# Fewer raw weight slots, a prepared bias table, and products on TensorE that nothing reads, in a streaming encoder layer

## The chip, the cores and the metric

The kernel runs on one core of a Trainium2 chip. A core has five engines that run their own instruction streams: TensorE (PE, with its weight loads listed as PEld), VectorE (DVE), ScalarE (ACT), GpSimd (POOL) and SyncE (SP), which here issues nearly all DMA transfers. The metric is the device time of one execution in microseconds. The kernel before took 1180.17 us, the median of three runs (1178.12 to 1184.04).

## The reference

One layer of an encoder: three groups of attention heads read the same normalised input through one input projection and are merged by one output projection. The call handles a prompt of 2048 rows and a sample batch of 8 x 16 = 128 rows, which have cached keys and values. The core of it:

```python
qa, ka, va, ga, qb, kb, vb, gb, qm, gm = _project(yp, g_pre[l], w_in[l])   # RMSNorm, then one matmul
oa = _band_attention(..., 8 chunks to the left, _relpos_bias(rel_bias_a[l], d), None)   # A: 6 heads x 64
ob = _band_attention(..., 2 chunks to the left, ALiBi, sink_b[l])                       # B: 6 q, 2 kv heads
om = _attn_core(qm, mk, mv, None, None, None)                                           # M: 4 heads, 256 tokens
yp = x + _rmsnorm(concat(oa*silu(ga), ob*silu(gb), om*silu(gm)) @ w_out[l], g_post[l])
```

In branch A a row of chunk c sees the keys of chunks c - 8 to c, 576 keys, and to each score a learned bias is added that depends on the head and on the distance, clipped at 128. The sample rows run through the same projections and attend to 512 cached keys and their own 16 (A), to 128 and 16 (B) and to 256 memory tokens (M). All is float32, D_MODEL is 1024.

## The kernel before, in words

**Precision and weights.** Each float32 product is done as three products of split numbers: a value is split in a high part and the low rest, and high x high, low x high and high x low are summed (`PASSES`). So each weight tile of 128x1024 is prepared by `load_w` (L145): SP starts a DMA into a raw tile (`wraw`, pool `wrawp`), ACT makes the high half (L153), and DVE and POOL in turn make the low half (L154) in a tile `whl`, of which there are three. The pool `wrawp` has three slots, and not for weights alone: the cached keys of the sample rows (`kta` L736, `ktb` L824) and two residual rows at the very end use the same ring. The slots are given out in the order in which the program asks for them, and a request waits until the last reader of the slot's former tile is done.

**Groups and order.** The prompt is worked on in 4 groups of 512 rows; group 0 carries the 128 sample rows too. In each group one lane of dense steps (projections to queries, keys and gates as `psT`, L213; to values, the memory's among them, and outputs as `psN`, L226) and one lane of attention steps are woven together: `DENSE` and `ATTENTION` list the steps, `AFTER` what must precede them, and `PACE` sets how much dense work is recorded per unit of attention. In group 0 the dense lane is V0 Pa0 Pa1 V1 Pb0 K0 and so on, the attention lane M0 M1 Sa0 Aa0 Sa1 Aa1 Sb0 Ab0: V are value weights, Pa and Pb the projections of a head pair, K0 the keys of branch B, Sa and Sb the sample rows' attention, Aa and Ab the prompt's. A scheduler then sets the order on each engine from costs that it assumes; each engine runs its own list in that order.

**The head.** `first_rows` (L477) loads the first 640 rows in eight blocks of 128 input features, scales each (`xn`, high part by ACT, L489, low by DVE, L490) and asks for the first two weights. `biases` (L349) loads the sinks and builds a row of 767 biases by distance for each head, which goes to DRAM (`e_d`). `bands` (L369) copies each head's row 128 times to DRAM (`skew_d`), so that a read with a row step of 767 instead of 768 gives a bias that depends on row minus column (`toeplitz`).

**Where the bias is read.** For the sample rows `sample_a` (L719) puts the bias of a head pair together from 17 small transfers (`nbs`). For the prompt `weigh` in `attn_a` loads a 128x640 tile for each head (`nbA`, L757); POOL then writes 1e30 into the two corners of 64x64 that a chunk may not see (L758, L759). DVE subtracts this bias from the scores. PSUM tiles of the tag `pt` (pool `p_t`) serve transposes and, in the head, some projections.

## Time and profile before

| What | Value |
|---|---|
| median of the runs | 1180.17 us (1178.12 to 1184.04) |
| the profiled execution | 1177.05 us, span 1175.3 us |
| mean granted TensorE clock | 0.987 |
| busy: PE, PEld | 1126.3 us (96%), 1019.6 us (87%) |
| busy: DVE, ACT, POOL | 810.9 us (69%), 729.4 us (62%), 301.1 us (26%) |
| instructions of POOL | 243, of them 48 memsets on `nbA` |
| PE products `psT` (L213) | 2400, 522.1 us busy |
| weight transfers `wraw` | 128 of 512 KB, median 3.6 us from issue to landing |

A timeline row gives the start, the length, the engine, the line with its operation, output and inputs with their shapes, how many instructions are taken together, and in brackets the idle time of the engine just before and what ended it. A stage window gives the busy time of each engine within a stretch of the span and the TensorE clock that was granted in it.

### The profile page before, as it was taken

To read this page: it belongs to the slowest core of one execution; us is meant where nothing else is said; L and a number is where in the kernel's file an instruction comes from. 1 tells how busy PE (TensorE), PEld (TensorE's weight loads), DVE (VectorE), ACT (ScalarE), POOL (GpSimd) and SP (SyncE) were. 2 spreads that over 40 slices of the span, in tenths; PEclk is the share of its full clock that TensorE was granted. 3 is DMA by queue.
4 is the path that set the end of the run, shared out by engine and by line. 5 is a ranking of instruction groups with operands and counts; after the bars stand their busy time and mean duration, and the time that the engine had idled before them with its cause. 6 is when DMAs were issued, how large, how long until landed. Compare 5 with 4: busy or idle time off the path is not lost.

```text
span 1175.3 us, 20987 instructions
## 1 busy us (share of the span) xinstructions
PE 1126.3 (96%) x7794; PEld 1019.6 (87%) x7794; DVE 810.9 (69%) x1875; ACT 729.4 (62%) x1688; POOL 301.1 (26%) x243
## 2 busy tenths in 40 slices
PE   7899999899899999999999999999999999999997
PEld 6889899799589988998789988988889988898797
DVE  7738766677775347677988337678987337678865
ACT  7646555666575566566886455567876456567762
POOL 4210210120321461221411451221411541212211
PEclk9999999899899999999999999999999999999899
DMA  7663445324721494233330394333321483232222
GB/s 274 221 226 136 155 158 206 113 83 132 266 95 43 159 332 167 92 108 116 116 95 24 108 368 164 93 124 104 113 94 37 125 297 97 77 115 84 76 68 100
DMA packets 62237, 163.42 MB, mean 139 GB/s; under 512 B 8108, under 2 KB 19378, under 8 KB 62136
## 3 DMA queue, kind: packets, MB, share of 16 engines
q1 hardware_dynamic: 58392, 152.66, 38.5%
q0 software_dynamic: 3744, 9.44, 2.7%
q8 instruction: 61, 1.00, 0.3%
q14 instruction: 40, 0.33, 0.1%
HBM read 140.95 MB, written 23.48 MB: 140 GB/s over the span
## 4 chain that ended last, share of the span: by engine, by line
PE 69%; DVE 10%; issue 8%; ACT 8%; DMA 3%; POOL 2%; SPq 1%; DVEq 0%; POOLq 0%; ACTq 0%
PE psT L213 31%; PE psN L226 20%; PE pt L273 4%; PE oa L286 4%; PE sa L267 4%; DVE sh L235 2%; ACT whl L153 1%; POOL whl L154 1%; PE ob L286 1%; DMA xt<-in_x_p 1%; DVE whl L154 1%; PE ss L384 1%; PE om L286 1%; DVE sbm L689 1%; PE so L420 1%
## 5 line engine op out<-in xcount | busy, mean ns | idle before, releaser
L213 PE MATMUL psT<-xn,whl 128*128 128x512 f32 (+2 forms) x2400 | 522.1, 367 | 13.7 <-ACT whl L153 5.7
L213 PEld LDWEIGHTS psT<-xn,whl 128*128 128x128 f32 x2400 | 408.3, 190 | 75.5 <-ACT whl L153 5.7
L154 POOL TENSOR_TENSOR whl<-wraw,whl 128x1024 fp32r<-128x1024 f32 x63 | 154.1, 2446 | 350.5 <-ACT whl L153 301.4
L226 PE MATMUL psN<-whl,sh 128*128 128x256 f32 x1296 | 164.0, 284 | 7.3 <-POOL whl L154 5.3
L226 PEld LDWEIGHTS psN<-whl,sh 128*128 128x128 f32 x1296 | 157.3, 190 | 10.0 <-POOL whl L154 5.7
L153 ACT ACTIVATE whl<-wraw 128x1024 fp32r<-128x1024 f32 (+1 forms) x132 | 138.3, 1047 | 26.1 <-PE psN L226 16.4
L226 PE MATMUL psN<-whl,xn 128*128 128x256 f32 x1080 | 145.1, 284 | 2.9 <-ACT stgN L652 1.1
L226 PEld LDWEIGHTS psN<-whl,xn 128*128 128x128 f32 x1080 | 134.4, 189 | 6.3 <-issue 1.6
L235 DVE TENSOR_TENSOR sh<-pt,sh 128x512 fp32r<-128x512 f32 (+2 forms) x206 | 122.2, 625 | 13.0 <-ACT sh L234 12.0
L234 ACT ACTIVATE sh<-pt 128x512 fp32r<-128x512 f32 (+2 forms) x206 | 103.6, 547 | 34.8 <-PE pt L273 26.4
L775 ACT ACTIVATE sba<-sba,sta 128x640 f32<-128x640 f32 (+2 forms) x96 | 73.1, 762 | 57.8 <-DVE sta L773 57.3
L154 DVE TENSOR_TENSOR whl<-wraw,whl 128x1024 fp32r<-128x1024 f32 (+1 forms) x69 | 94.9, 1375 | 19.4 <-ACT whl L153 18.7
L665 POOL TENSOR_TENSOR mo<-sums,gr 128x256 f32<-128x256 f32 (+1 forms) x38 | 37.6, 989 | 234.7 <-DVE sums L294 208.8
L773 DVE CUSTOM_DVE_ANT_0 sba<-sa,nbA 128x640 f32<-128x640 f32 (+2 forms) x96 | 70.7, 737 | 28.8 <-PE sa L267 27.8
L286 PE MATMUL oa<-sh 128*128 128x256 f32 (+1 forms) x504 | 75.1, 281 | 1.8 <-DVE sh L235 0.9
L286 PEld LDWEIGHTS oa<-sh 128*128 128x128 f32 x504 | 68.4, 192 | 5.0 <-DVE sh L235 1.9
L273 PE MATMUL pt<-ident,sba 128*128 128x128 f32 x420 | 64.6, 276 | 3.4 <-DVE sh L235 2.6
L526 DVE TENSOR_TENSOR mo<-psN,gpost 128x256 f32<-128x256 f32 x52 | 21.9, 422 | 61.6 <-ACT junk L525 61.4
L778 DVE TENSOR_SCALAR sba<-sba,sta 128x640 f32<-128x640 f32 (+2 forms) x96 | 59.4, 619 | 2.7
L267 PE MATMUL sa<-sh,qr 128*128 128x320 f32 (+2 forms) x240 | 52.0, 327 | 4.4 <-DVE sta L773 2.3
L273 PEld LDWEIGHTS pt<-ident,sba 128*128 128x128 f32 x420 | 48.7, 141 | 7.2 <-DVE sh L235 3.4
L858 ACT ACTIVATE sbb<-sbb,stb 128x256 f32<-128x256 f32 (+1 forms) x96 | 47.3, 494 | 11.4 <-DVE stb L856 11.2
(285 smaller groups left out, 1572.8 us busy)
## 6 DMA issues: line engine op xcount, KB each, us to landing
wraw<-in_wt SPq DMA_DIRECT2D x128, 512.0 KB, 3.6
xr<-in_x_p SPq DMA_DIRECT2D x16, 512.0 KB, 5.3
nbA<-skew_d SPq DMA_DIRECT2D x24, 320.0 KB, 2.9
vta<-in_cva SPq DMA_DIRECT2D x12, 512.0 KB, 5.0
xt<-in_x_p SPq DMA_DIRECT2D x12, 512.0 KB, 4.9
out_y_p<-mo SPq DMA_DIRECT2D x12, 512.0 KB, 4.0
vctx<-sh SPq DMA_DIRECT2D x9, 512.0 KB, 5.0
kctx<-sh SPq DMA_DIRECT2D x9, 512.0 KB, 4.1
```

The source lines that it names most:

```text
L153: act.activation(hl[:, 0, m], raw[:, m], AF.Copy)
L154: eng.tensor_tensor(hl[:, 1, m], raw[:, m], hl[:, 0, m].bitcast(F32), ALU.subtract)
L213: pe.matmul(ps[:, :n], w[:, a, k * 128:(k + 1) * 128], src[:, b, k, c0:c0 + n], start=(i == 0), stop=(i == 23))
L226: pe.matmul(ps[:, :256], stat(a, k), w[:, b, (k % 4) * 256:(k % 4 + 1) * 256], start=(k == ks[0] and i == 0), stop=(k == ks[-1] and i == 2))
L234: act.activation(hi, src, AF.Copy)
L235: eng.tensor_tensor(lo, src, hi.bitcast(F32), ALU.subtract)
L267: pe.matmul(out[:, c:c + n], q[:, part, qc:qc + 128], kt[:, h, kc:kc + n], start=part == h, stop=part != h)
L273: pe.transpose(pt[:, i * 128:(i + 1) * 128], b, ident)
L286: pe.matmul(o[:, oc:oc + w], v, pt[:, part, c:c + w], start=(first and i == 0), stop=(i == n - 1), skip_group_check=True)
L773: dve.tensor_tensor_reduce(sb[:, :nk], s[:, c0:c0 + nk], nb[h][:, 640 - nk:], 1.0, 3.0e38, ALU.add, ALU.min, st[:, e:e + 1])
L775: act.activation(sb[:, :nk], sb[:, :nk], AF.Exp, bias=st[:, e:e + 1], scale=-1.0, accum_out=st[:, 2 + e:3 + e])
L778: dve.tensor_scalar(sb[:, :nk], sb[:, :nk], st[:, 4 + e:5 + e], 0.5, ALU.mult, ALU.mult)
```

## The change

It has four parts.

1. `wrawp` has two slots instead of three.
2. A PSUM tile `idle` is made, and PE runs ten products of the 128x128 ones tile with itself into it (`WARM`), and eight products 128x384 on the first block of `xn` (`FILL`). Nothing reads the tile.
3. `biases` is cut in two. The part that builds the rows of biases comes first of all, so that its DMA (`er`) is the first on SP; the rows go to `e_d` behind `first_rows`; the sinks have a function of their own; `bands` moves from behind the memory attention to right behind the load of the memory's rows.
4. `masks` is new. POOL fills a tile once with 1e30, and two DMAs write it into `skew_d` at the places that the two 64x64 corners of each head are read from, so that the 48 memsets on `nbA` go. 15 DMAs build the sample rows' bias of three head pairs in DRAM (`sbias_d`), and `sample_a` then loads each by one. So 51 small transfers become 3 + 15 + 2.

The numbers of the weights, products and splits stay as they are. From about the first third of the span on the order of PE is unchanged up to the tail.

The order changes at three places. The first is the head. POOL's rows from the scale of the memory rows (`nstm`) to the first gated merges (`mo<-sums,gr`), before and then now:

```order
L163 TENSOR_TENSOR nstm<-nstm,expo 128x2
L154 TENSOR_TENSOR whl<-wraw,whl 128x1024
L758 MEMSET nbA 64x64
L759 MEMSET nbA 64x64
L154 TENSOR_TENSOR whl<-wraw,whl 128x1024
L758 MEMSET nbA 64x64
L759 MEMSET nbA 64x64
L154 TENSOR_TENSOR whl<-wraw,whl 128x1024 x3
L665 TENSOR_TENSOR mo<-sums,gr 128x4x128
```

```order
L166 TENSOR_TENSOR nst_251<-nst_251,expo 128x5
L384 MEMSET big 128x384
L166 TENSOR_TENSOR nstm<-nstm,expo 128x2
L157 TENSOR_TENSOR whl<-wraw,whl 128x1024 x6
L698 TENSOR_TENSOR mo<-sums,gr 128x4x128 x2
L698 TENSOR_TENSOR mo<-sums,gr 128x2x128 x2
```

The memsets between the splits have gone, and one memset of `big` stands ahead. PE's first rows, as they are now:

```order
L632 MATMUL idle<-ones 128x128 x10
L518 MATMUL idle<-xn 128x384 x8
L216 MATMUL psT<-xn,whl 128x384
L216 MATMUL psT_301<-xn,whl 128x256
L216 MATMUL psT<-xn,whl 128x384
L216 MATMUL psT_301<-xn,whl 128x256
L216 MATMUL psT<-xn,whl 128x384
```

Both kinds of added product stand ahead of the first real product; `psT` and `psT_301` are the two column ranges of the first projection.

The second place is the step V1 of group 0, with the second sample pair's attention (`ss<-kta`). PE before, from the last queries and keys ahead of it, and then now:

```order
L213 MATMUL psT<-xn,whl 128x256 x16
L226 MATMUL psN<-whl,xn 128x256 x3
L426 MATMUL spt<-ident,ssb 128x128
L273 MATMUL pt<-ident,sba 128x128 x6
L267 MATMUL sa<-sh,qr 128x512 x2
L226 MATMUL psN<-whl,xn 128x256 x16
L273 MATMUL pt<-ident,sba 128x128
L226 MATMUL psN<-whl,xn 128x256 x5
L286 MATMUL oa<-sh 128x256
L226 MATMUL psN<-whl,xn 128x256 x14
L267 MATMUL sa<-sh,qr 128x384 x2
```

```order
L216 MATMUL psT<-xn,whl 128x256 x6
L451 MATMUL spt<-ident,ssb 128x128
L276 MATMUL pt<-ident,sba 128x128 x6
L270 MATMUL sa<-sh,qr 128x512 x2
L289 MATMUL oa<-sh 128x256
L276 MATMUL pt<-ident,sba 128x128
L289 MATMUL oa<-sh 128x256
L289 MATMUL oa<-sh 128x128 x2
L276 MATMUL pt<-ident,sba 128x128
L270 MATMUL sa<-sh,qr 128x384 x2
```

The value products (`psN`) that stood between the attention's rows have gone from here. They now follow on the second scores on the cached keys; PE a little further down, now:

```order
L409 MATMUL ss<-kta,qd_122 32x512 x2
L289 MATMUL oa<-sh 128x256
L289 MATMUL oa<-sh 128x128 x2
L229 MATMUL psN<-whl,xn 128x256 x4
L409 MATMUL ss<-mo,qd_122 32x512 x2
L412 MATMUL ss<-ksm,qd_122 128x64
L229 MATMUL psN<-whl,xn 128x256 x20
```

SP at the same place, from the cached keys of that pair on, before and then now:

```order
L744 DMA vta<-in_cva 128x1024
L737 DMA kta<-in_ckaT 128x1024 x2
L152 DMA wraw<-in_wt 128x1024
L436 DMA mo<-in_ckaT 128x4x256 x2
L631 DMA out_akTs<-ksm 128x128
L152 DMA wraw<-in_wt 128x1024
L714 DMA kctx_126<-sh 256x1x512
L436 DMA mo<-in_ckaT 128x4x256
```

```order
L155 DMA wraw<-in_wt 128x1024
L764 DMA kta<-in_ckaT 128x1024 x2
L461 DMA mo<-in_ckaT 128x4x256 x2
L664 DMA out_akTs<-ksm 128x128
L747 DMA kctx_127<-sh 256x1x512
L771 DMA vta<-in_cva 128x1024 x2
L461 DMA mo<-in_ckaT 128x4x256
L754 DMA nbs<-sbias_d 128x576
L771 DMA vta<-in_cva 128x1024 x2
L784 DMA nbA<-skew_d 128x640 x2
L155 DMA wraw<-in_wt 128x1024
```

One weight transfer followed on the two loads of keys at once, and a second soon after; now no weight transfer stands between those and the bias of the next attention.

The third place is the first local attention (`sb`, step Ab0) beside the projections Pb. PE before, and then now:

```order
L213 MATMUL psT<-xn,whl 128x256
L267 MATMUL sb__2521<-sh,qr 128x128 x2
L267 MATMUL sb__2521<-sh,qr 128x256 x4
L286 MATMUL oa<-sh 128x256 x6
L286 MATMUL oa<-sh 128x128 x2
L273 MATMUL pt<-ident,sba 128x128 x5
L267 MATMUL sb__2521<-sh,qr 128x256 x2
L286 MATMUL oa<-sh 128x256
L384 MATMUL ss<-ktb,qd_121 32x128 x4
L387 MATMUL ss<-ksm,qd_121 128x64
```

```order
L216 MATMUL psT<-xn,whl 128x256 x24
L270 MATMUL sb__2520<-sh,qr 128x128 x2
L270 MATMUL sb__2520<-sh,qr 128x256 x4
L186 MATMUL rb<-dg,ones 128x128
L216 MATMUL psT<-xn,whl 128x384 x17
L186 MATMUL rb<-dg,ones 128x128 x2
L270 MATMUL sb__2520<-sh,qr 128x256 x2
L186 MATMUL rb<-dg,ones 128x128
L216 MATMUL psT<-xn,whl 128x384 x7
L216 MATMUL psT<-xn,whl 128x256 x22
L409 MATMUL ss<-ktb,qd_121 32x128 x4
```

The scores `sb` were followed by attention alone; now rows of 17, 7 and 22 products of projections stand among them.

The diff:

```diff
--- before.py
+++ after.py
@@ -49,6 +49,8 @@
          "M0 M1 Aa0 Aa1 Ab0 Ab1 Ab2 Aa2",
          "M0 M1 Aa0 Aa1 Ab0 Ab1 Ab2 Aa2")
 
+WARM, FILL = 10, 8
+
 PACE = 0.3
 
 PIECE = 6
@@ -68,7 +70,7 @@
     pe, act, dve, pool, sp = nc.tensor, nc.scalar, nc.vector, nc.gpsimd, nc.sync
 
     cst = ctx.enter_context(tc.tile_pool(name="cst", bufs=1))
-    wrawp = ctx.enter_context(tc.tile_pool(name="wrawp", bufs=3))
+    wrawp = ctx.enter_context(tc.tile_pool(name="wrawp", bufs=2))
     whlp = ctx.enter_context(tc.tile_pool(name="whlp", bufs=3))
     xp = ctx.enter_context(tc.tile_pool(name="xp", bufs=2))
     nbp = ctx.enter_context(tc.tile_pool(name="nbp", bufs=3))
@@ -138,6 +140,7 @@
 
     skew_d = drp.tile([6, 128 * 768], F32, name="skew_d")
     e_d = drp.tile([6, 768], F32, name="e_d")
+    sbias_d = drp.tile([3, 128, 576], F32, name="sbias_d")
     kctx_d = [drp.tile([128, 2, 512], F32, name=f"kctx{i}") for i in range(6)]
     vctx_d = [drp.tile([128, 4, 256], F32, name=f"vctx{i}") for i in range(6)]
 
@@ -346,8 +349,22 @@
 
         return skew_d[h, 127:127 + 767 * 128].rearrange("(p c) -> p c", c=767)[:n, c0:c1]
 
+    def dram(ap, offset, *dims):
+
+        return bass.AP(tensor=ap.tensor, offset=ap.offset + offset, ap=[list(d) for d in dims])
+
     def biases():
 
+        er = nbp.tile([128, 640], F32, tag="nb", name="er")
+        sp.dma_start(out=er[0:6, 0:257], in_=rel_rev)
+        ee = gr[:, 768:1536]
+        dve.memset(ee[0:6, 0:768], 0.0)
+        dve.tensor_scalar(er[0:6, 0:257], er[0:6, 0:257], -1.0, None, ALU.mult)
+        dve.tensor_scalar(ee[0:6, 0:511], ee[0:6, 0:511], er[0:6, 0:1], None, ALU.add)
+        dve.tensor_copy(ee[0:6, 511:767], er[0:6, 0:256])
+        return ee
+
+    def sinks():
         sp.dma_start(out=sk, in_=sink.partition_broadcast(128))
         sp.dma_start(out=selt, in_=sel)
         dve.tensor_scalar(nsk, sk, -1.0, None, ALU.mult)
@@ -357,18 +374,26 @@
                                      ALU.mult, ALU.add)
         dve.tensor_scalar(nsks, sks, -1.0, None, ALU.mult)
 
-        er = nbp.tile([128, 640], F32, tag="nb", name="er")
-        sp.dma_start(out=er[0:6, 0:257], in_=rel_rev)
-        ee = gr[:, 768:1536]
-        dve.memset(ee[0:6, 0:768], 0.0)
-        dve.tensor_scalar(er[0:6, 0:257], er[0:6, 0:257], -1.0, None, ALU.mult)
-        dve.tensor_scalar(ee[0:6, 0:511], ee[0:6, 0:511], er[0:6, 0:1], None, ALU.add)
-        dve.tensor_copy(ee[0:6, 511:767], er[0:6, 0:256])
-        sp.dma_start(out=e_d, in_=ee[0:6, 0:768])
-
     def bands():
         for h in range(6):
             sp.dma_start(out=skew_d[h].rearrange("(p c) -> p c", c=768), in_=e_d[h].partition_broadcast(128))
+
+    def masks():
+
+        big = nbp.tile([128, 640], F32, tag="nb", name="big")
+        pool.memset(big[:, 0:384], BIG)
+        for p, c in ((0, 576), (64, 0)):
+            sp.dma_start(out=dram(skew_d, 127 + 767 * p + c, (767, 64), (98304, 6), (1, 64)),
+                         in_=big[p:p + 64, 0:384].rearrange("p (h c) -> p h c", h=6))
+        for pr in range(3):
+            sp.dma_start(out=sbias_d[pr, :, 512:576], in_=mask_new)
+            for h in range(2):
+                at = (128 * pr + 16 * h) * 576
+                src = (2 * pr + h) * 98304 + 127
+                sp.dma_start(out=dram(sbias_d, at, (32 * 576, 4), (576, 16), (1, 512)),
+                             in_=dram(skew_d, src, (0, 4), (767, 16), (1, 512)))
+                sp.dma_start(out=dram(sbias_d, at + 512, (32 * 576 + 16, 4), (576, 16), (1, 16)),
+                             in_=dram(skew_d, src + 512, (0, 4), (767, 16), (1, 16)))
 
 
     def sample_attn(f, Q, G, kts, vts, ncach, new, bias, skcol):
@@ -489,6 +514,8 @@
             act.activation(xnT[0][:, 0, k], xm[:, k], AF.Copy, scale=gpre[:, k:k + 1])
             dve.scalar_tensor_tensor(xnT[0][:, 1, k], xm[:, k], gpre[:, k:k + 1], xnT[0][:, 0, k].bitcast(F32),
                                      ALU.mult, ALU.subtract)
+            for _ in range(FILL if k == 0 else 0):
+                pe.matmul(idle[:, :384], xnT[0][:, 0, 0, :128], xnT[0][:, 0, 0, :384], start=True, stop=True)
         for k in range(KB):
             total = sums[k % 2]
             t = total if k < 2 else nbp.tile([128, 640], F32, tag="nb", name="sq1")
@@ -599,24 +626,30 @@
             dve.scalar_tensor_tensor(G[:, c0:c0 + n], G[:, c0:c0 + n], 1.0, ps[:, :n], ALU.add, ALU.mult)
         return G
 
+
+    idle = p_t.tile([128, 512], F32, tag="pt", name="idle")
+    for i in range(WARM):
+        pe.matmul(idle[:, :128], ones, ones, start=True, stop=True)
     for t in qd:
         pool.memset(t, 0.0)
     for q in qslots[:2]:
         zero_rows(q)
+    ee = biases()
     xm, sums, wq, wg = first_rows()
-    biases()
+    sp.dma_start(out=e_d, in_=ee[0:6, 0:768])
+    sinks()
     rs, rs_rows = first_scales(xm, sums)
     qg = [(*run(block_q(0, 6, wq)), run(block_g(0, 6, wg)))]
     w7 = [weights("q", 7), weights("g", 7)]
     sp.dma_start(out=gmem, in_=g_mem)
     mT = memory_load()
+    bands()
     mst = memory_rows(mT)
     qg.append((*run(block_q(0, 7, w7[0])), run(block_g(0, 7, w7[1]))))
     memory_keys(mst)
+    masks()
     for p in range(2):
         sample_m(p, *qg[p][1:])
-    bands()
-
     bctx = None
     for g in range(NG):
         def block_k(p, dst, outT, outTs, lastn):
@@ -718,13 +751,7 @@
 
         def sample_a(pr, Q, G, ksm, vsm):
             bias = nbp.tile([128, 640], F32, tag="nb", name="nbs")
-            sp.dma_start(out=bias[:, 512:576], in_=mask_new)
-            for h in range(2):
-                for b in range(4):
-                    r = 32 * b + 16 * h
-                    sp.dma_start(out=bias[r:r + 16, 0:512], in_=toeplitz(2 * pr + h, 16, 0, 512))
-                    sp.dma_start(out=bias[r:r + 16, 512 + 16 * b:528 + 16 * b],
-                                 in_=toeplitz(2 * pr + h, 16, 512, 528))
+            sp.dma_start(out=bias[:, 0:576], in_=sbias_d[pr])
             kt, vt = {}, {}
 
             def kts(hf, b):
@@ -755,8 +782,6 @@
                     for hh in range(2):
                         t = nbp.tile([128, 640], F32, tag="nb", name="nbA")
                         sp.dma_start(out=t, in_=toeplitz(2 * pr + hh, 128, 0, 640))
-                        pool.memset(t[0:64, 576:640], BIG)
-                        pool.memset(t[64:128, 0:64], BIG)
                         nb.append(t)
                 st = stp.tile([128, 16], F32, tag="st", name="sta")
                 for i in (i0, i0 + 1):
```

## The prediction

> **What bounds the kernel now.** I read the page's busy shares first, then the chain of waits, then the timeline and the stage windows around every place where TensorE (PE) waits. Times in a timeline row are the start, the length, and in brackets the idle time before it with its releaser.
>
> ```profile
> span 1175.3 us, 20987 instructions
> PE 1126.3 (96%) x7794; PEld 1019.6 (87%) x7794; DVE 810.9 (69%) x1875; ACT 729.4 (62%) x1688; POOL 301.1 (26%) x243
> PE 69%; DVE 10%; issue 8%; ACT 8%; DMA 3%; POOL 2%; SPq 1%; DVEq 0%; POOLq 0%; ACTq 0%
> ```
>
> PE is busy 96% of the span, so 1175.3 − 1126.3 = 49 us of idle time is all that better cover could return, plus the stretches in which PE works at a lower clock. The change leaves the products that count as they are, so its worth is decided in those holes. The windows below show two of them in group 0 (columns: length, then busy time and count of PE, PEld, DVE, ACT, POOL, the granted clock, the DMA share, GB/s). In each, a thin stretch is followed by one of some 6.8 us at clock 0.50.
>
> ```profile
> 53.90:55.90 2.00, 0.00 (x0) 0.00 (x0) 1.18 (x1) 1.50 (x3) 0.29 (x2) 1.00 0.98 311
> 55.90:58.30 2.40, 0.01 (x1) 0.01 (x1) 2.37 (x2) 0.00 (x0) 2.40 (x2) 0.50 0.54 211
> 58.30:62.70 4.40, 4.40 (x20) 4.40 (x21) 1.34 (x4) 0.73 (x2) 0.17 (x2) 0.50 0.67 214
> 206.00:212.90 6.90, 3.15 (x20) 2.19 (x18) 5.88 (x15) 6.38 (x18) 3.10 (x2) 1.00 0.52 165
> 212.90:219.70 6.80, 6.48 (x37) 5.60 (x38) 5.87 (x26) 3.66 (x16) 1.91 (x2) 0.50 0.54 175
> ```
>
> **The change part by part.** The sum has six terms, each against the profiled execution's 1177.05 us.
>
> *The memsets leave POOL.* The stall at 53.9 has this cause:
>
> ```profile
> 42.96 2.40 POOL L154 TENSOR_TENSOR whl<-wraw,whl 128x1024 fp32r<-128x1024 f32 x1 [4.36 <-ACT whl L153]
> 55.48 0.15 POOL L758 MEMSET nbA<- 64x64 f32 x1 [10.11 <-DMA nbA<-skew_d]
> 55.90 2.34 POOL L154 TENSOR_TENSOR whl<-wraw,whl 128x1024 fp32r<-128x1024 f32 x1
> 58.30 6.26 PE L226 MATMUL psN<-whl,sh 128*128 128x256 f32 x34 [4.42 <-POOL whl L154]
> 66.87 1.44 PE L226 MATMUL psN<-whl,xn 128*128 128x256 f32 x10 [0.25 <-POOL whl L154]
> wraw<-in_wm SPq DMA_DIRECT2D x4, 512.0 KB, 4.6
> ```
>
> POOL stood 10.11 us behind a bias transfer, the low half of the last memory weight (wm3) behind it, and PE waited 4.42 us; 4.4 us of half clock cost another 2.2. Now POOL only splits there, and the queue that had stood behind it is free. But with two raw slots wm3 loads only once wm1's split has ended: 42.96 + 2.40 = 45.4, plus 4.6 to land, 1.06 for the high half (the ACT split's mean, row further down) and 2.40 for the low: 53.4, just before the 53.9 at which PE ran dry. The slot then serves the second value weight: 53.4 + 4.6 + 1.06 + 2.4 = 61.5, where before PE got it at 66.87. I take −5.4; the ends are −6.6 (4.4 + 2.2, all of it) and −3 (each of two loads 1.2 us late). The distance row now goes out first on SP, ahead of the first rows, for one issue (0.42 us below): +0.4. Together −5.
>
> *Products that nothing reads.* What the head looks like:
>
> ```profile
> 1.19 0.42 SPq L485 DMA_DIRECT2D gpre<-in_g_pre  x1
> 3.87 0.83 ACT L489 ACTIVATE xn<-mo,gpre 128x640 fp32r<-128x640 f32 x1 [1.64 <-DMA gpre<-in_g_pre]
> 5.71 1.97 PE L213 MATMUL psT<-xn,whl 128*128 128x384 f32 x6 [5.71 <-ACT whl L153]
> 9.54 6.57 PE L213 MATMUL psT<-xn,whl 128*128 128x384 f32 x24 [1.86 <-ACT xn L489]
> 16.42 4.46 PE L213 MATMUL psT<-xn,whl 128*128 128x384 f32 x28 [0.30 <-DVE whl L154]
> 21.14 2.69 PE L213 MATMUL psT<-xn,whl 128*128 128x384 f32 x16 [0.26 <-DVE xn L490]
> ```
>
> Twenty-four products take 6.57 us, then 28 take 4.46: a slow start up to about 15 us, 274 ns a product against 159. In the order both kinds of added product stand ahead of the first real one. The ten need only the ones; the eight need the first block's high half, there at 3.87 + 0.83 = 4.70, and take 8 × 0.344 to 8 × 0.578 us (means of 128x384 products at the two speeds, next rows), so the first real product starts at about 7.5 to 9.3 instead of 5.71.
>
> ```profile
> L213 PE MATMUL psT<-xn,whl 128*128 128x384 f32 x9 | 4.6, 578 | 1.9 <-ACT xn L489 1.9
> L213 PE MATMUL psT<-xn,whl 128*128 128x384 f32 x16 | 3.4, 344 | 0.3 <-DVE whl L154 0.3
> ```
>
> The cover is the feed: at 16.42 and 21.14 PE had used up all that DVE had made and waited 0.30 and 0.26. If the added products bring the full clock sooner, thirty real ones (the 6 and the 24) take 30 × 0.159 = 4.8 us and end by 9.3 + 4.8 = 14.1, in time for 16.1; then PE waits longer for DVE, and nothing is won. Ends: −3.4, if the feed itself moves up and half of the 6.57 us comes back, and +1.7, if the clock stays slow: 9.3 + 30 × 0.274 = 17.5 against 16.1, and the 0.30 of the old wait. I take 0, since two waits show the feed ahead of PE as the limit.
>
> The Trainium skill, "TensorE: Matmul & The Clock Gate", "Part 1: The HAM clock gate", puts full clock after about 3.4 us of sustained work. By that rule the real products would all run fast, which is the first of the two cases here; the gain would still need a faster feed.
>
> *Two raw slots around the first value weights.* Both slots are now taken by the cached keys of the second sample pair until its scores have read them.
>
> ```profile
> 100.41 8.35 SPq L737 DMA_DIRECT2D kta<-in_ckaT  x2
> ...
> 147.74 0.37 SPq L152 DMA_DIRECT2D wraw<-in_wt  x1
> 153.68 0.33 SPq L152 DMA_DIRECT2D wraw<-in_wt  x1
> 165.46 0.62 PE L384 MATMUL ss<-kta,qd 128*32 128x512 f32 x2
> 174.99 1.04 PE L384 MATMUL ss<-kta,qd 128*32 128x512 f32 x2
> 149.80:165.50 15.70, 15.70 (x136) 15.36 (x137) 11.71 (x35) 9.00 (x24) 1.34 (x5) 1.00 0.46 158
> 149.80:165.50 15.70, 11.94 (x85) 10.86 (x85) 2.08 (x6) 2.17 (x6) 1.00 0.46 158
> 149.80:175.00 25.20, 25.20 (x206) 23.77 (x204) 17.78 (x49) 15.33 (x37) 4.52 (x7) 1.00 0.48 166
> 149.80:175.00 25.20, 17.05 (x120) 15.33 (x120) 2.78 (x8) 3.35 (x9) 1.00 0.48 166
> 149.80:175.00 25.20, 2.55 (x15) 2.23 (x13) 0.42 (x1) 0.00 (x0) 1.00 0.48 166
> L153 ACT ACTIVATE whl<-wraw 128x1024 fp32r<-128x1024 f32 x3 | 3.2, 1059 | 2.2 <-DMA wraw<-in_wt 1.8 <-PE psN L226 0.4
> L154 DVE TENSOR_TENSOR whl<-wraw,whl 128x1024 fp32r<-128x1024 f32 x2 | 2.4, 1218 | 1.5 <-ACT whl L153 1.5
> wraw<-in_wt SPq DMA_DIRECT2D x128, 512.0 KB, 3.6
> ```
>
> Before, the third slot let weights load while the keys lay in the other two, and PE was full: of 25.2 us, 17.05 went to value products (the second and fourth window are those of psN alone, columns PE, PEld, DVE, ACT) and 2.55 to psT (the fifth), leaving 25.2 − 17.05 − 2.55 = 5.6 us of attention. In the new order no value product stands until the second scores are out. So count from T, the place at 149.8. DVE needs 11.71 − 2.08 − 1.22 (one split) = 8.4 us of attention work to reach the first scores; with PE's own 0.62 and a handover, T + 9.4 frees the first slot, and by the same subtraction over 25.2 us (17.78 − 2.78 − 0.42 − 2.4 = 12.2) T + 12 frees the second. Its load takes 0.35 + 3.6 + 1.06, and POOL's 2.4: T + 19.4. In that time PE has the 5.6 us of attention, 12 value products on the first weight (12 × 17.05/120 = 1.7), and about 2.2 of the attention that would have come later. Idle: 19.4 − 9.5 = 9.9. A thin stretch that long brought the half clock at 206 to 212.9, where 3.15 of 6.9 us were busy; I charge 2.2 for it, between 0 and 3.4 (half of 6.8). Together +12; ends +7 (the chain of scores 3 us quicker, no half clock) and +17 (below).
>
> The Trainium skill, the same title, "HAM oscillation — how this bites in real kernels", has the clock drop only after a gap of over about 3.4 us. By it this term would lose its 2.2 and the sum 2. The trace disagrees: the longest gap before 212.9 was 2.03.
>
> *The first local attention.* What was thin at 206 to 212.9:
>
> ```profile
> 210.76 0.50 PE L267 MATMUL sb__2521<-sh,qr 128*128 128x256 f32 x2 [2.03 <-DVE sh L253]
> ```
>
> In the new order, key and query products stand between those scores in rows of 17, 24 and more. The old loss was 6.9 − 3.15 = 3.75 idle and 6.8/2 = 3.4 of half clock, 7.15. The dense work delayed at T is what fills it. I take −6; ends −7.2 and 0, if T's delay falls on the keys too.
>
> *The end of group 0.* The next group's first weights need slots that the third pair's keys hold until 301.45 (their last scores):
>
> ```profile
> 301.45 0.69 PE L387 MATMUL ss<-ksm,qd 128*128 128x64 f32 x2
> 303.64 2.52 PE L213 MATMUL psT<-xn,whl 128*128 128x512 f32 x7
> 308.42 1.08 PE L420 MATMUL so<-vta,spT 128*32 128x128 f32 x32
> ```
>
> 301.45 + 0.35 + 3.6 + 1.06 = 306.5 against 303.64 before; PE has 1.9 us of other work, such as the last row's, to put ahead: +1, ends 0 and +4.
>
> *The rest.* 51 small bias transfers become 20, and the sink work moves; all of it lies under PE's work: 0, ends −1 and +1. From 420 us on the order of PE, to the start of the tail, is that of before, and there a raw slot is needed for 3.6 + 1.06 + 2.4 = 7.1 us in each 24 × 0.344 = 8.3 that PE spends on a tile, so two slots are enough.
>
> Sum: −5 + 0 + 12 − 6 + 1 + 0 = +2, so 1179. The median shown is 1180.17 − 1177.05 = 3.1 above its profiled execution: 1182.
>
> **The rivals.** *The hole at T is shallow* (0.25): the scores come 3 us earlier, no half clock follows, and the stall at 206 goes altogether. −6.6 + 7 − 7.15 + 0 = −6.8: 1173. For it: ACT and DVE are freed of splits there. Against: scores, softmax and their transposes take turns between engines, and a busy sum is a floor.
>
> *The raw slots decide* (0.26): without dense work between, each turn of DVE, ACT and PE shows in full, and the second scores come at T + 16. The second value weight is ready at T + 23.4; idle 23.4 − 9.5 = 13.9, and 3.4 of half clock: +17.3. The group's end costs 2.5. −5 + 17.3 − 6 + 2.5 = +8.8: 1189. It decides from about T + 14. For it: both slots are held by name, and no other source of weights exists. Against: DVE's sum says T + 12.
>
> *The added products pay* (0.05): −3.4 on the sum, 1179. Against: the two waits on DVE. It needs the early full clock and a feed that keeps up.
>
> *They do not do what they say* (0.03): the clock stays low through the added products, +1.7: 1184.
>
> **How the numbers follow.** The forecast's own case has 0.41 and 1177 to 1187. A difference under 0.5%, 5.9 us, is about what a measurement of this kernel cannot tell from none, so "same" is 1174.3 to 1186.1. Faster: most of the shallow hole, 0.22, and 0.04 of the forecast's edge: 0.26. Slower: 0.22 of the raw-slot case, 0.06 of the edge, 0.02 of others: 0.30. Same: 0.44. The range takes in both neighbours: 1172 to 1192.
>
> **What would show it.** No POOL wait of 10 us before 55, and the second value weight's products near 61. At the head, added products from 1 us on, real ones from 7.5 to 9.3, and waits on DVE before 21. A PE gap of about 10 us starting near 145, ended by a weight split whose load was issued right behind scores on the cached keys, then maybe clock 0.50. No half clock where the first local scores run. I am wrong if that gap is under 5 us or over 16, if weights load beside the keys after all, or if the head ends over 3 us apart from the old one.

## The result and the profile after

The changed kernel takes 1185.47 us (median of 20 runs, 1181.06 to 1189.19), the kernel before 1180.23 us (median of 20, 1177.13 to 1184.04): a ratio of 1.0051, with a 95% interval of 1.0040 to 1.0062. (The ratio on record is not the quotient of the medians; that one is 1.0044.) So it is slower by about 0.5%, clear of zero, and right at the bound that the prediction set between "same" and "slower", 5.9 us. The forecast was 1182 with a range of 1172 to 1192: the time lies in it, 3.5 us above the forecast.

The profiled execution of the changed kernel took 1188.58 us and that of before 1177.05, so the two traces differ by 11.5 us where the medians differ by 5.2. About half of what a comparison of these two traces shows is the spread between runs.

The page after: the span and the busy shares.

```profile
span 1186.6 us, 20916 instructions
PE 1135.0 (96%) x7822; PEld 1023.6 (86%) x7822; DVE 812.0 (68%) x1875; ACT 729.8 (62%) x1688; POOL 291.7 (25%) x196
```

POOL has 47 instructions less, and PE 28 more: the eight products and the ten, each of which the trace lists as two.

To see where the time goes, I gave each of PE's products (the added ones left out) its median duration in the trace of before; together they make 1068 us. The table lists, for each stretch of this work, how many us later (+) or earlier (−) than in the trace of before a kernel got through it. The stretches end, in the trace of before, at about 33, 128, 228, 340, 360 and 1168 us. How a product's length is counted moves an entry by up to 0.5 us.

```
stage, by work done (us)            0-20  20-100  100-180  180-270  270-290  290-1068   all
                                    head  memory  V1, Ab0  end g0   turn     groups 1-3
the changed kernel                  -0.4   +1.8    -3.6     +6.7     +3.8     +3.1     +11.4
c  no added products                +0.1    0.0    -3.6     +8.2     -1.0     +0.5      +4.2
l  1 + 1 added                       0.0   -0.4    -3.4     +6.4     -0.9     +4.7      +6.3
j  2 + 2 added                      +0.5   -1.0    -4.2     +4.2     +4.9     +3.5      +7.9
f  12 + 8 added                     -0.3   -1.4    -1.7     +7.0     +3.6     +4.9     +12.2
g  10 + 10 added                    +1.2   -0.4    -0.9     +8.2     +2.3     +2.3     +12.6
i  20 + 8 added                     +1.4   +0.6    -3.1     +5.9     -0.9     +3.0      +6.9
b  before, two slots                +0.7   +0.2    -3.1     +5.7     -1.0     -0.2      +2.2
d  bias part, three slots            0.0   +1.5    +1.1     +1.1     +6.0     +0.8     +10.4
a  d with the added products        -0.1   +0.5    +1.7     +0.4     +5.6     +2.2     +10.2
e  before, added products           -0.1   -0.5    +1.3     +8.9     +1.0     +4.1     +14.8
h  bias part, own slot for keys     -0.5   -0.2    -3.0     +1.2     -0.9     +3.5      +0.3
k  h, small bias loads              -0.1   +0.2    -1.1     +0.1     -0.9     +1.8       0.0
```

*The memory weights.* Timeline of the changed kernel, SP, POOL and PE, around the old stall at 54:

```profile
42.78 5.87 SPq L395 DMA_DIRECT2D sbias_d<-skew_d  x3
49.32 0.45 SPq L155 DMA_DIRECT2D wraw<-in_wm  x1
55.31 2.34 POOL L157 TENSOR_TENSOR whl<-wraw,whl 128x1024 fp32r<-128x1024 f32 x1 [7.74 <-ACT whl L156]
58.44 5.80 PE L229 MATMUL psN<-whl,sh 128*128 128x256 f32 x34 [2.65 <-DVE mkn L339]
68.80 1.59 PE L229 MATMUL psN<-whl,xn 128*128 128x256 f32 x10 [1.11 <-ACT stgT L301]
```

POOL no longer waits behind a bias transfer. But the load of wm3 is issued at 49.32, since on SP it stands behind transfers that build the table and wait for one another to land (6.5 us in four waits between 24 and 58 us, and 2.8 us once for the masks); its low half ends at 57.65, where it ended at 58.24 before.

*The added products and the start.*

```profile
1.05 4.40 PE L632 MATMUL idle<-ones 128*128 128x128 f32 x20 [1.05 <-DVE ones L125]
5.35 1.66 PE L518 MATMUL idle<-xn 128*128 128x384 f32 x8
6.85 1.06 PE L216 MATMUL psT<-xn,whl 128*128 128x384 f32 x6
9.12 0.56 PE L216 MATMUL psT<-xn,whl 128*128 128x384 f32 x2 [1.21 <-ACT xn L514]
16.00 7.42 PE L216 MATMUL psT<-xn,whl 128*128 128x384 f32 x47 [0.81 <-DVE whl L157]
```

The first real products run at the fast rate (six in 1.06 us, 1.97 before), and then PE waits for its feed, four times before 14 us.

*V1, with two raw slots.* PE and SP, and two stage windows:

```profile
159.29 0.62 PE L409 MATMUL ss<-kta,qd 128*32 128x512 f32 x2
160.38 0.33 SPq L155 DMA_DIRECT2D wraw<-in_wt  x1
164.11 1.05 PE L409 MATMUL ss<-kta,qd 128*32 128x512 f32 x4
165.49 0.69 PE L229 MATMUL psN<-whl,xn 128*128 128x256 f32 x4
167.34 2.60 PE L229 MATMUL psN<-whl,xn 128*128 128x256 f32 x20
...
150.90:165.50 14.60, 12.69 (x77) 8.00 (x76) 11.61 (x39) 9.82 (x25) 0.73 (x1) 1.00 0.55 181
165.50:180.00 14.50, 13.67 (x148) 11.35 (x148) 9.41 (x24) 7.05 (x18) 3.12 (x2) 1.00 0.70 231
```

The weight's load goes out right behind the first scores on the keys, as forecast. But of the 29.1 us of the two windows PE is idle for only 2.7, and the clock stays at 1.00.

*The end of group 0.* PE, SP, and the window:

```profile
302.75 2.19 PE L409 MATMUL ss<-kta,qd 128*32 128x512 f32 x8
303.85 0.33 SPq L155 DMA_DIRECT2D wraw<-in_wt  x1
312.08 3.64 PE L216 MATMUL psT<-xn,whl 128*128 128x512 f32 x8 [2.16 <-DVE whl L157]
...
300.00:320.00 20.00, 16.06 (x104) 11.22 (x103) 13.35 (x32) 11.70 (x24) 6.45 (x4) 0.91 0.85 292
```

Here the shared ring costs what the forecast put at V1: the second half's keys and the next group's first weights follow one another through two slots.

*The turn from group 0 to group 1.* PE and ACT of the changed kernel, then of the run without added products (c):

```profile
347.89 5.07 PE L229 MATMUL psN<-whl,sh 128*128 128x256 f32 x41
352.80 1.05 PE L289 MATMUL oa<-sh 128*128 128x256 f32 x8
357.40 2.00 ACT L950 ACTIVATE sh<-mo 128x1024 fp32r<-128x1024 f32 x2 [1.66 <-POOL mo L698]
358.50 0.39 PE L229 MATMUL psN<-whl,sh 128*128 128x256 f32 x1 [1.95 <-ACT sh L950]
359.45 7.53 PE L229 MATMUL psN<-whl,sh 128*128 128x256 f32 x47 [0.56 <-ACT sh L950]
...
360.10:363.40 3.30, 3.30 (x18) 3.30 (x17) 2.12 (x7) 1.12 (x6) 0.00 (x0) 0.50 0.00 0
```

```profile
346.65 1.05 PE L289 MATMUL oa<-sh 128*128 128x256 f32 x8
347.54 1.84 PE L216 MATMUL psT<-xn,whl 128*128 128x512 f32 x7
349.22 2.99 PE L229 MATMUL psN<-whl,sh 128*128 128x256 f32 x24
351.27 2.01 ACT L950 ACTIVATE sh<-mo 128x1024 fp32r<-128x1024 f32 x2 [0.30 <-POOL mo L698]
```

The last eight products of group 0's attention in branch A (`oa`) feed a chain: ACT and DVE sum them, POOL gates them (`mo`), ACT and DVE split the rows (`sh`), and the output products of group 1's first step (`psN`) need the split rows. In the changed kernel the scheduler put `oa` behind 41 of those output products; the first 48 use other rows, the 49th waits for the chain, 1.95 and 0.56 us, and some 3.4 us at clock 0.50 follow (the window row). Without the added products `oa` stands ahead, and nothing waits.

### The profile page after: what moved, and what is told of

Read it like the earlier page. It is cut to its first block, busy times and chain, and to the rows that moved or that the text cites. A ratio compares the mean times of both kernels' runs of the same rounds, so it can differ in the third digit from the quotient of the medians.

```text
span 1186.6 us, 20916 instructions
## 1 busy us (share of the span) xinstructions
PE 1135.0 (96%) x7822; PEld 1023.6 (86%) x7822; DVE 812.0 (68%) x1875; ACT 729.8 (62%) x1688; POOL 291.7 (25%) x196
## 5 line engine op out<-in xcount | busy, mean ns | idle before, releaser
L216 PE MATMUL psT<-xn,whl 128*128 128x512 f32 (+2 forms) x2400 | 516.6, 365 | 11.2 <-DVE whl L157 3.0
L216 PEld LDWEIGHTS psT<-xn,whl 128*128 128x128 f32 x2400 | 404.0, 188 | 73.8 <-DVE whl L157 3.7
L157 DVE TENSOR_TENSOR whl<-wraw,whl 128x1024 fp32r<-128x1024 f32 (+1 forms) x69 | 99.1, 1437 | 22.9 <-ACT whl L156 22.9
```

Of the source, the lines that this page charges most:

```text
L157: eng.tensor_tensor(hl[:, 1, m], raw[:, m], hl[:, 0, m].bitcast(F32), ALU.subtract)
L216: pe.matmul(ps[:, :n], w[:, a, k * 128:(k + 1) * 128], src[:, b, k, c0:c0 + n], start=(i == 0), stop=(i == 23))
```

## The experiments

Ratios are to the kernel before on the same chip, with 95% intervals; its median there was 1180.15 us for a to h, 1179.26 for i, j and k, 1179.85 for l.

**Which part costs it: a, b, c, d.** The edits, in this order:

```diff
-    wrawp = ctx.enter_context(tc.tile_pool(name="wrawp", bufs=2))      # a: on the changed kernel
+    wrawp = ctx.enter_context(tc.tile_pool(name="wrawp", bufs=3))
-    wrawp = ctx.enter_context(tc.tile_pool(name="wrawp", bufs=3))      # b: on the kernel before
+    wrawp = ctx.enter_context(tc.tile_pool(name="wrawp", bufs=2))
-WARM, FILL = 10, 8                                                     # c: on the changed kernel
+WARM, FILL = 0, 0                                                      # d: the edits of a and c together
```

> The changed kernel with three raw slots again (bias table and added products kept). TensorE's order is then nearly that of before. Theory R (the two raw slots cost the time, at the cached keys): 1175 to 1181 us, at or a little below before, with no gap over 1 us at a weight behind the keys near 312 us. Rival H (the head's bias transfers and the added products cost it): it stays at 1183 to 1188. Rival N (the 5 us are spread, from the order of groups 1 to 3): about half, 1182 to 1184.

Measured: 1187.30 us, 1.0054 (1.0039 to 1.0070). Theory R falls; the time is the one that rival H named.

> The kernel before with two raw slots as the only edit. Theory R: it is as slow as the changed kernel or a little slower, 1184 to 1190, with the wait for a weight behind the cached keys near 312 us. Rival H: within 2 us of before. My prediction's own term for the slots was +7 net (hole +12, local attention -6, end of the group +1), which would be 1187.

Measured: 1181.52 us, 1.0008 (0.9994 to 1.0023). Two slots alone cost nothing that can be told, and my own +7 for them fails.

> The changed kernel without the products that nothing reads. If they are hidden by the feed, as predicted, within 2 us of the changed kernel: 1183.5 to 1187.5. If they pay, 3 us slower than the changed kernel: 1188 to 1190. If they hinder, 2 us faster or more: below 1183.5. First real products at about 5.7 us again, 24 of them at the slow rate.

Measured: 1180.50 us, 0.9999 (0.9986 to 1.0012). The changed kernel without its added products is as fast as the kernel before: "they hinder" holds.

> The bias part alone: three raw slots, no added products. My term for it was -5 (the stall at 54 us goes): 1175. Theory R with a head that gains nothing, as the trace of the changed kernel looks (its last memory weight's low half ended at 57.65 against 58.24): 1179 to 1181. Rival H: the table's transfers hold up weights on SP, 1183 or more.

Measured: 1186.63 us, 1.0050 (1.0032 to 1.0068). PE and ACT of this run:

```profile
51.90 5.92 PE L229 MATMUL psN<-whl,sh 128*128 128x256 f32 x48
60.08 1.44 PE L229 MATMUL psN<-whl,xn 128*128 128x256 f32 x10 [0.20 <-POOL whl L157]
64.94 1.06 ACT L156 ACTIVATE whl<-wraw 128x1024 fp32r<-128x1024 f32 x1 [6.72 <-DMA wraw<-in_wt]
68.08 4.78 PE L229 MATMUL psN<-whl,xn 128*128 128x256 f32 x21 [6.56 <-ACT stgT L301]
```

The stall at 54 is gone as costed: 48 products in a row, and the second value weight's products at 60.08 instead of 66.87. But then ACT, in order, stands 6.72 us behind the next weight's transfer, up to 64.94; the copy `stgT` that frees PE's PSUM tile is behind it, and PE waits 6.56, up to 68.08. The wait moved from POOL's queue to ACT's. The time is in the range of rival H, 1183 or more, but not for its reason: the table has only +1.5 up to 128 us for the head.

The four do not add up: two slots 0, bias part +6, both 0, both and the added products +5. On three slots the added products change next to nothing: a has d's order on all engines but for 17 places of PE at the head, and the ratios are 1.0054 and 1.0050. What goes with the time is in the table's column of the turn: +6.0 and +5.6 in d and a, +3.8 in the changed kernel, −1.0 in b and c. In d and a too, 8 `oa` products stand behind 48 output products. That made a new theory, O: the order at the turn costs it, and the added products matter because they shift the scheduler's reckoning.

**Is it the order or the products: f, g, i, j, l.** All are the changed kernel with one line edited:

```diff
-WARM, FILL = 10, 8
+WARM, FILL = 12, 8      # f; g: 10, 10; i: 20, 8; j: 2, 2; l: 1, 1
```

> The changed kernel with 12 + 8 added products instead of 10 + 8. TensorE's order then comes out, apart from the added products, as in the run without any (two places of 7521 differ): at the turn from group 0 to group 1 the last local attention's products (oa) stand ahead of the first output products. Theory O (the 5 us come from that order at the turn, and not from the added products): 1179.5 to 1182, as without the products. Rival P (the added products cost it by themselves, or by their effect on the clock): 1185 or more, as the changed kernel.

Measured: 1184.88 us, 1.0046 (1.0028 to 1.0063). Its trace shows `oa` behind 41 output products: it did not have the order that I gave it, and so is a second run of the changed kernel's order.

> The changed kernel with 10 + 10 added products. TensorE's order is word for word that of the changed kernel: the last 8 oa products of group 0 stand behind 41 output products. Theory O: 1184.5 to 1187, the wait for the split of the mixed rows near 358 us and a half-clock stretch behind it. Rival P: the same or a little more. With the run of 12 + 8 it tells the two apart.

Measured: 1185.44 us, 1.0049 (1.0032 to 1.0066), as O and P both allow.

> The changed kernel with 20 + 8 added products. The run with 12 + 8 did not have the order that its expectation gave it: its trace shows the 8 oa products behind 41 output products, as in the changed kernel. This one has the most added products of all, and an order of TensorE that differs from that of the run without any in two places of 7521, both among the first products: at the turn the oa products stand ahead. Theory O (the order at the turn costs the 5 us, the added products nothing): 1179 to 1182, plus at most 2 for ten more products at the start. Rival P (the added products cost it): 1186 or more.

Measured: 1186.13 us, 1.0057 (1.0039 to 1.0074), against O. The trace shows no loss at the turn (−0.9 in the table). Its order is c's and l's: on ACT, DVE, POOL and SP no place differs in the traces, on PE two at the head. So here 0.58% between c and i comes with the added products and without a change of order at the turn. The trace shows a late start:

```profile
1.05 7.67 PE L632 MATMUL idle<-ones 128*128 128x128 f32 x40 [1.05 <-DVE ones L125]
8.47 1.64 PE L518 MATMUL idle<-xn 128*128 128x384 f32 x8
9.95 3.27 PE L216 MATMUL psT<-xn,whl 128*128 128x384 f32 x20
```

The first real product is at 9.95 instead of 6.53 in c, and the table has +1.4 and +0.6 for it. That is 2 of the 6.5 us by which its median stands above c's; the profiled execution, 1183.88 us, was the shortest of its runs. The granted clock is worth some 2 more by an estimate (0.990 against 0.992, medians over the runs, of 1180 us). The rest stays open, and with it what twenty products cost by themselves.

> The changed kernel with 2 + 2 added products, too few to warm anything. TensorE's order is, without them, exactly that of the changed kernel: at the turn the oa products stand behind 41 output products. Theory O: 1184 to 1187, as the changed kernel, with a wait of about 2 us for the split of the mixed rows near 358 us. Rival P: 1180 to 1182, near the run without added products.

Measured: 1182.68 us, 1.0036 (1.0024 to 1.0049), a little under O's range, with an interval clear of the run without added products.

> The changed kernel with 1 + 1 added products. It has two added products less than the run with 2 + 2, and TensorE's order flips to that of the run without any (no place of 7521 differs): at the turn the oa products stand ahead. Theory O (the order at the turn costs 3 to 5 us): 1179 to 1181.5, as without products, and no wait over 1 us between 350 and 362 us. Rival (the orders are worth the same, and the runs with 2 + 2 and more are slow for another reason, such as the start): 1182 to 1184.

Measured: 1180.01 us, 0.9993 (0.9980 to 1.0007). PE at the turn of j, then of l:

```profile
347.82 1.06 PE L289 MATMUL oa<-sh 128*128 128x256 f32 x8
353.53 0.46 PE L229 MATMUL psN<-whl,sh 128*128 128x256 f32 x1 [1.94 <-ACT sh L950]
354.48 8.56 PE L229 MATMUL psN<-whl,sh 128*128 128x256 f32 x47 [0.49 <-ACT sh L950]
```

```profile
344.43 1.03 PE L289 MATMUL oa<-sh 128*128 128x256 f32 x8
346.98 2.99 PE L229 MATMUL psN<-whl,sh 128*128 128x256 f32 x24
```

j and l differ by two added products and by the order that came of them, which is the changed kernel's in j and c's in l; the intervals do not touch, and j loses 4.9 us at the turn where l gains 0.9. l has no wait over 1 us between 350 and 362, as O said. So the order is worth 0.43% (1.0036 − 0.9993), about 5 us, with next to no added products; by the medians, each less that of before on its chip, it is 3.3 us. (In the traces PE's two orders differ in 342 places of 7794: 148 at the end of group 0 and the turn, 103 at the next turn, 69 in the tail and 22 at the head. In the table l loses 2.2 us more just ahead of the turn, and 1.2 more behind it, so not all of the 5.8 at the turn stays. That the loss sits at the turn is read from the traces; no run changes the order there alone.) The changed kernel's 10 + 8 lie at 1.0051 with j's order: 0.15%, or 1.8 us, above j, and the intervals overlap: whether that many products cost anything more is open. f, g and j have the changed kernel's order on every engine; no run has 10 + 8 products and c's order on two slots.

**The added products on the kernel before: e.**

```diff
+    idle = p_t.tile([128, 512], F32, tag="pt", name="idle")
+    for i in range(WARM):
+        pe.matmul(idle[:, :128], ones, ones, start=True, stop=True)
...
+            for _ in range(FILL if k == 0 else 0):
+                pe.matmul(idle[:, :384], xnT[0][:, 0, 0, :128], xnT[0][:, 0, 0, :384], start=True, stop=True)
```

> The kernel before with the added products as the only edit. My term for them was 0: 1178.5 to 1182. In its order no oa product of group 0 stands behind an output product, so theory O expects no cost at the turn either. Rival P: 1185. If they pay: 1177.

Measured: 1195.00 us, 1.0124 (1.0104 to 1.0143). Every expectation missed it. Nothing is lost at the head (−0.6 by 128 us); 8.9 us go at the end of group 0:

```profile
334.25 0.54 PE L288 MATMUL oa<-sh 128*128 128x256 f32 x3
339.55 7.30 PE L215 MATMUL psT<-xn,whl 128*128 128x512 f32 x24 [4.77 <-DVE gr L603]
```

In the order that came out here the last projections of the next group stand in blocks of 24 behind the attention instead of among it, and one waits for the gate of the one before. Again the loss is at an order 300 us behind the edit; no run with another order tests this one.

**A version from this: h, k.** The cached keys get a slot of their own, so that weights pass by them; k also keeps the small bias loads of before, so that no transfer that builds a table stands ahead of a weight on SP.

```diff
+    ktp = ctx.enter_context(tc.tile_pool(name="ktp", bufs=1))                # h and k, on c
-                        t = wrawp.tile([128, 1024], F32, tag="wraw", name="kta")
+                        t = ktp.tile([128, 1024], F32, tag="kta", name="kta")
...
-        for pr in range(3):                                                  # k: no sbias_d
-            sp.dma_start(out=sbias_d[pr, :, 512:576], in_=mask_new)
...
-            sp.dma_start(out=bias[:, 0:576], in_=sbias_d[pr])                # k: the 17 transfers of before
```

> The bias part with two raw slots for weights and one slot of its own for the cached keys of the sample rows (as much memory as three raw slots), no added products. The end of group 0 should lose what the shared ring cost there (in the runs with two shared slots the lag grows by 6 to 8 us from 230 to 340 us): if it does and the rest is as in the run without added products, 1174 to 1177. If the cost there is from the second pair of key tiles itself (one slot, loaded one after the other), 1180 to 1184. In its order the last oa products stand ahead of all output products, so theory O expects no wait at the turn.

Measured: 1179.75 us, 0.9994 (0.9978 to 1.0011), between its two expectations. The end of group 0 falls from +8.2 in c to +1.2, as expected, but groups 1 to 3 give 3.5 of it back in this trace.

> A version made from what the runs showed: the masks are written into the bias rows in DRAM by two transfers (no memsets on POOL), the sample rows' bias is loaded by the small transfers of before (so that no transfer that builds a table stands on SP ahead of a weight), two raw slots for weights and one of its own for the cached keys, no added products, and an order at the turn with the oa products ahead. If the head's stall goes (5 us) and the key slot returns what it did in its own run: 1174 to 1177. If the head's wait only moves on to ACT's queue, as in the bias part alone: 1179 to 1181.

Measured: 1175.67 us, 0.9968 (0.9953 to 0.9982): 3.6 us faster than the kernel before, the only one clear of it. At the turn PE is full, and in the head a wait on ACT's queue is left:

```profile
345.00:365.00 20.00, 20.00 (x172) 20.00 (x172) 12.22 (x24) 10.32 (x31) 2.94 (x2) 1.00 0.17 44
...
64.23 6.91 PE L229 MATMUL psN<-whl,xn 128*128 128x256 f32 x36 [3.79 <-ACT stgT L301]
```

Its trace is not faster than that of before (0.0 in the table; its 1177.29 us stand 1.6 above its median, the 1177.05 of before 3.2 below), so the stage that gives the 3.6 us isn't shown. The time met the first expectation, 1174 to 1177, while its condition, a head without a wait, did not come in its trace.

## Why the prediction was right, and where its steps were not

The time, 1185.5, was in the range and 3.5 us above the forecast; a loss had 0.30 and no change 0.44, and the result lies on the line between. That the sum was near is luck: in the trace three places came out 6 to 7 us above their terms and one 10 us below, and these errors cancel in part.

- **The memsets leave POOL: −5 in the sum, +1.4 by 128 us in this trace** (head and memory together; −1.7 to +2.0 in c, l, j, f, g and i, which have the same bias part). The mechanism is shown by d: with three slots the stall at 54 goes and the second value weight comes 6.8 us earlier. What I called "just before the 53.9 at which PE ran dry" failed: I had the slot free at 45.4 (in the trace 47.6), let wm3 load at once and did not ask what stood ahead of it on SP. The table-building transfers did; it went out at 49.32, and its low half was done at 57.65 instead of 53.4. And when the stall does go, ACT's queue takes it over (d).
- **Products that nothing reads: 0 in the sum, −0.4 at the head.** Right for the reason given: full rate from the first real product on, and then waits for the feed. "The cover is the feed" holds. The times were off: the first real product came at 6.85, not at 7.5 to 9.3, since the lengths of 344 and 578 ns that I multiplied by 8 overlap from one product to the next (all eight took 1.66 us). What I left out is what the added products do to the order.
- **Two raw slots around the first value weights: +12, and the first local attention: −6.** Together +6 in the sum, −3.6 in the trace. The times of the chain were near: first scores at T + 9.4 forecast, 159.29 − 150.96 = 8.3 in the trace (T is at 150.96 there), the second at T + 12 and 13.2. The idle time was not: 9.9 forecast, 2.7 measured, and by the mark that I had set ("under 5 us") this step was wrong. The step "leaving 5.6 us of attention" failed: alone on PE, 77 products of that attention keep it busy 12.69 of 14.6 us, 165 ns each, where my subtraction had given 51 of them 3.8 us (15.70 − 11.94, 136 − 85 in the rows of before), 74 ns each; and 24 value products ran before the second weight could be there (SP issued it at 165.21), not 12. So no half clock came either. The local attention then ran full, as forecast: 39.42 of 40 us busy.

```profile
200.00:240.00 40.00, 39.42 (x289) 36.97 (x289) 23.10 (x76) 21.36 (x62) 6.52 (x4) 1.00 0.27 87
```

- **The end of group 0: +1 in the sum, +6.7 in the trace**, above my end of +4. All runs with two shared slots lose 4 to 8 there, those with three slots or an own one 0.1 to 1.2 (e, whose order is another, apart). I counted one load behind the last scores; the second half's keys themselves had to wait for the first half's scores (SP issued them at 299.06), and the weights came behind those.
- **"The rest: 0"** hid the turn, +3.8 in this trace and 3 to 5 us by j against l, and groups 1 to 3, +3.1, which differ by as much between traces of one order (j +3.5, f +4.9, g +2.3). I had looked at the order at three places and not at this fourth one, where no edited line runs. (That two slots are enough there rests on 8.3 us for a tile, again a sum of lengths that overlap: in the trace of before 24 products of 128x512 take 5.87 us, at 329.70. Two slots still give a weight every 7.1/2 = 3.6 us.)

Of the rivals, "the hole at T is shallow" was right that the hole is shallow and brings no half clock, though the second scores came later than forecast and not 3 us earlier; its 1173 failed at the memsets, at the end of group 0 and at the turn. "The raw slots decide" ended on the right side for another reason: b shows that the slots alone cost nothing.

## What to carry to other kernels

Where a scheduler orders the instructions, an edit is also a new order everywhere behind it: compare the whole order, look for the last producer of a chain that now stands behind work which doesn't need it, and test an edit against one that does the same work with another order before giving it a cause. A wait taken off one in-order queue shows what the next queue has in front: ask of ACT and SP, not only of the engine that waited. It need not be the order alone: i kept the good order and was slow all the same. And one profile against one profile said 11.5 us here where 20 runs against 20 said 5.2.

## What was not expected of the hardware

A wait of the same length is followed by half clock in one execution and not in another. At the turn from group 1 to group 2 the traces of before and of h have the same order of PE, with a wait of 1.29 and 1.28 us ahead of the same products. PE, then windows, of before and then of h:

```profile
613.11 1.72 PE L273 MATMUL pt<-ident,sba 128*128 128x128 f32 x8 [1.29 <-DVE sh L235]
617.31 0.55 PE L226 MATMUL psN<-whl,sh 128*128 128x256 f32 x2
...
608.88:612.29 3.41, 2.80 (x23) 2.43 (x21) 3.41 (x7) 3.19 (x7) 0.14 (x1) 1.00 0.43 108
612.29:615.70 3.41, 2.40 (x16) 1.87 (x17) 3.35 (x9) 2.31 (x9) 0.80 (x3) 1.00 0.42 147
615.70:619.12 3.42, 2.36 (x19) 2.13 (x18) 3.39 (x7) 3.23 (x7) 0.10 (x1) 1.00 0.00 0
```

```profile
609.41 1.71 PE L277 MATMUL pt<-ident,sba 128*128 128x128 f32 x8 [1.28 <-DVE sh L239]
615.16 3.05 PE L230 MATMUL psN<-whl,sh 128*128 128x256 f32 x24
...
608.21:611.62 3.41, 2.03 (x13) 1.49 (x14) 3.35 (x9) 2.68 (x11) 0.34 (x1) 1.00 0.53 162
611.62:615.03 3.41, 3.41 (x18) 3.41 (x18) 3.38 (x6) 2.67 (x4) 0.41 (x1) 0.50 0.00 0
```

In h 3.41 us at clock 0.50 follow, in before none. From the wait's end to the first `psN` h takes 5.75 us and before 4.20, so the stretch costs 1.55 us; half of 3.41, 1.7 us, is the estimate for one that PE fills. What differs is where the wait falls. In each trace the clock changes only at steps of 3.41 us from its other changes, and the windows above are such steps: in h the wait lies in one, which leaves PE 2.03 us busy in it, in before it is shared by two, with 2.80 and 2.40. In the fourteen traces the clock fell to half behind 58 of the 61 windows of full clock in which PE was busy less than half of the time, behind 30 of 70 from there to two thirds, and behind 5 of 4416 above. So a shift of the same wait by a microsecond or two can decide whether half clock follows.

By the Trainium skill, "TensorE: Matmul & The Clock Gate", "Part 1: The HAM clock gate", the activity window is free-running, which fits; its rule of thumb ("HAM oscillation — how this bites in real kernels") against idle gaps of more than about 3.4 us does not cover the wait of 1.28 us in h that was followed by half clock. The mean granted clock, as the median over the runs, was 0.987 for the kernel before, 0.9905 for the changed one and 0.981 to 0.983 for a and d, which with the span makes an estimated 15, 11 and 20 to 22 us lost to it. b and c, at 0.9915 and 0.992, gained 5 to 6 us of clock on the kernel before and came out even, so they lost about as much elsewhere.
